# Attention with one set of products with v per head instead of two, a scaled negated maximum on ScalarE, and a last tile stored in two parts

## The chip, the cores and the metric

The kernel runs on one core of one Trainium2 chip. The metric is the device time in microseconds of one execution of the program. Five engines work side by side, each through its own queue of instructions in order: TensorE (PE, with its weight loads shown apart as PEld), VectorE (DVE), ScalarE (ACT), GpSimd (POOL) and SyncE (SP, which here only issues DMAs). They wait for one another through semaphores.

## What is computed

A trunk of two residual layers on 512 tokens of width 1024. Layer 0 mixes tokens with a gated linear attention, layer 1 with softmax attention; each is followed by a gated feed-forward block with a width-3 convolution over tokens. The change touches the softmax attention (8 query heads, 2 key/value heads, 128 wide) and the very last step of the second feed-forward block. The attention of the reference, cut:

```python
q = apply_rope(rmsnorm(q, q_norm), cos, sin)
k = apply_rope(rmsnorm(k, k_norm), cos, sin)
def block(q_blk):                       # 128 queries
    s = jnp.einsum('bkgqd,bksd->bkgqs', q_blk, k) * scale
    p = jax.nn.softmax(s, axis=-1)
    return jnp.einsum('bkgqs,bksd->bkgqd', p, v)
...
x = x + o @ w_out
x = x + conv_ffn(rmsnorm(x, norm_ffn[i]), ...)
```

## The kernel before

Everything is kept feature-major: a tile holds 128 features by 512 tokens. To keep float32 accuracy at the faster matmul type, each operand is split into a high part (rounded by an ACT copy) and a low part (the difference, made by DVE), and a product is three matmuls: high by high, high by low, low by high. `mm3` (line 251) issues these three, so lines 253 to 255 stand for most matmuls of the profile. Weights arrive as `raw` tiles of 1 MB on SP's queue; `Weights.make` (114) splits them by an ACT copy `wh` and a DVE subtraction `wl` (140, 141), or, for the attention's weights, by two ACT copies (123, 124) and an accumulating DMA that POOL issues (133). `wh` and `wl` have three buffers each.

A tile framework assigns buffers, inserts all waits, and reorders the instructions by its own cost model. The program's source order is thus only its priority; the order on each engine is what the built program shows. PSUM has eight banks, named by tag: `acc` (3), `s` (2), `pt` (2), `po` (1).

The attention (function `attention`, line 604) works by blocks of 128 queries, 32 blocks in all: four blocks (`j`) for each of eight heads (`h`). Block number t runs through these steps:

- `scores` (736): three matmuls of 512 columns give the scores `s` of 128 queries by 512 keys in an `s` bank. DVE takes the row maximum `mx` (745) and multiplies it by the row's scale and by -1 to `nb` (746). ACT computes exp with scale and bias `nb` into `p` and sums the row (748).
- `shares` (751): DVE takes the reciprocal `rc` of the sum (753) and scales `p` (754).
- `turn` (757), four blocks later: TensorE transposes the four 128x128 parts of `p` into a `pt` bank (766). ACT copies the bank to `pth` (769), DVE subtracts to `ptl` (770). A pair of these tiles holds two blocks: 4 key parts by 256 queries.
- `mix` (772), six blocks later and after every second block: twelve matmuls of 256 columns multiply v (`vh`, `vl`) with half a head's `pth`, `ptl` into one half of the `po` bank. After the second half, ACT and DVE split `po` into the head's output tile `oT` (670, 671).

Between these steps a plan (`Q_STEPS`, `Q_READY`, `O_STEPS`) places pieces of other work. These are the projections of the next pairs of query heads (`qpair`, 694, into `A` and `B`, with the head norms `hs` and `hr`, the scales `qsc`, the rotations `rt` on DVE and their sums `ry` on POOL at 663 and 664, and the split of `q` on ACT and DVE at 670 and 671), and the first parts of the output projection (`out_steps`, 292, into `op`). `hr` is a power on POOL (197).

The big tiles (`big`, 22 buffers) hold `pth`, `ptl`, `q`, `k` and the `oT` of heads 0 to 3; the `oT` of heads 4 to 7 use the eight `xhl` buffers that held the normalised input. The last feed-forward block adds each `dn` bank to the residual `x` on DVE (597) and stores it by a DMA on SP's queue (601).

Of the kernel before, what the change touches and what calls it, by code (L numbers as in the profile page):

```python
# [8 lines left out]
F32 = mybir.dt.float32  # L9
F32R = mybir.dt.float32r  # L10
U8 = mybir.dt.uint8
AF = mybir.ActivationFunctionType
ALU = mybir.AluOpType

P = 128
S = 512
D = 1024
KC = D // P
NT = S // P
# [12 lines left out]
LAGS = (4, 6)  # L32
# [14 lines left out]
def hybrid_encoder_kernel(  # L47
# [21 lines left out]
    pe, act, dve, pool, sync = nc.tensor, nc.scalar, nc.vector, nc.gpsimd, nc.sync  # L69
# [8 lines left out]
    def nm(s):  # L78
        uid[0] += 1
        return f"{s}{uid[0]}"  # L80
# [3 lines left out]
    def bank(tag, n):  # L84
        return pp.tile([P, S], F32, tag=tag, bufs=PS[tag], name=nm(n))

    def pair(tag, bufs, dt, n):
        return sp.tile([P, 2 * S], dt, tag=tag, bufs=bufs, name=nm(n))

    def big(dt, n):  # L90
        return pair("g", 22, dt, n)

    def tmp(tag, n, w=S):
        return sp.tile([P, w], F32, tag=tag, bufs={"u": 4, "t": 6, "sq": 3}[tag], name=nm(n))

    def tiny(w, n, tag="tiny"):
        return sp.tile([P, 8], F32, tag=tag, bufs={"tiny": 36, "tiny2": 4}[tag], name=nm(n))[:, :w]


    x = [cp.tile([P, S], F32, name=f"x{c}") for c in range(KC)]  # L100
# [150 lines left out]
    def mm3(ps, wh, wl, mh, ml, start, stop):  # L251

        mm(ps, wh, mh, start=start, stop=False)  # L253
        mm(ps, wh, ml, start=False, stop=False)  # L254
        mm(ps, wl, mh, start=False, stop=stop)  # L255
# [10 lines left out]
    def feature_tile(*a):  # L266
        for _ in feature_steps(*a):
            pass
# [290 lines left out]
    def ffn(layer, norm, cw, nxt):  # L559
        hl = []  # L560
        for m in range(FC):
            res, pss = [], []
            for t in range(2):
                ps = bank("s" if t else "acc", "up")
                feature_tile(*W.half(up[layer], 2 * m + t), norm.hl, ps)
                pss.append(ps)
                if m == 0 and t == 0:
                    norm.tokens()
                elif m == 0:
                    norm.rows()  # L570
            for t in range(2):
                ps = pss[t]
                cc = ((layer * 2 + t) * FC + m) * 4
                w = lambda i: cw[:, cc + i : cc + i + 1]
                u = tmp("u", "u")
                dve.tensor_tensor(u, ps, norm.R, ALU.mult)  # L576
                y = tmp("t", "y")
                act.activation(y, u, AF.Identity, scale=w(1), bias=w(3))  # L578
                dve.scalar_tensor_tensor(y[:, 1:], u[:, : S - 1], w(0), y[:, 1:], ALU.mult, ALU.add)  # L579
                dve.scalar_tensor_tensor(y[:, : S - 1], u[:, 1:], w(2), y[:, : S - 1], ALU.mult, ALU.add)  # L580
                res.append(y)
            act.activation(res[1], res[1], AF.Silu)  # L582
            dve.tensor_tensor(res[0], res[0], res[1], ALU.mult)
            t = big(F32R, "gu")
            act.activation(t[:, :S], res[0], AF.Copy)
            dve.tensor_tensor(t[:, S:], res[0], t[:, :S].bitcast(F32), ALU.subtract)
            hl.append((t[:, :S], t[:, S:]))
        cur = None
        for c in range(KC):
            ps = bank("acc", "dn")  # L590
            for k in range(FC):
                u = c * FC + k
                if u % 8 == 0:
                    cur = W.half(down[layer], u // 8)
                sl = slice((u % 8) * P, (u % 8 + 1) * P)
                mm3(ps, cur[0][:, sl], cur[1][:, sl], *hl[k], k == 0, k == FC - 1)
            dve.tensor_tensor(x[c], x[c], ps, ALU.add)
            if nxt is not None:
                nxt.chunk(c)
            else:  # L600
                sync.dma_start(out[c * P : (c + 1) * P, :], x[c])


    def attention(norm, nxt):
# [64 lines left out]
        def split(y, tile_):  # L669
            act.activation(tile_[:, :S], y, AF.Copy)  # L670
            dve.tensor_tensor(tile_[:, S:], y, tile_[:, :S].bitcast(F32), ALU.subtract)

        def whole(gen):
            while True:
                try:
                    next(gen)
                except StopIteration as e:
                    return e.value
# [39 lines left out]
        ps = [bank("acc" if j < 2 else "pt", "av") for j in range(NT)]  # L718
# [7 lines left out]
        vh, vl = big(F32R, "vh"), big(F32R, "vl")  # L726
        for j in range(NT):
            sl = slice(j * 256, (j + 1) * 256)
# [4 lines left out]
        oh = [None] * QH  # L733
        probs, pts, pos = {}, {}, {}

        def scores(h, j):

            qt, sc, e = heads[h]
            kt = kk[h // 4]
            js = slice(j * P, (j + 1) * P)  # L740
            s = bank("s", "s")
            mm3(s, qt[:, js], qt[:, S + j * P : S + (j + 1) * P], kt[:, :S], kt[:, S:], True, True)
            scj = sc[:, 2 * j + e : 2 * j + e + 1]
            mx, nb, sm, rc = (tiny(1, n) for n in ("mx", "nb", "sm", "rc"))
            dve.reduce_max(mx, s, axis=mybir.AxisListType.X)
            dve.tensor_scalar(nb, mx, scj, -1.0, ALU.mult, ALU.mult)
            p = tmp("t", "p")
            act.activation(p, s, AF.Exp, scale=scj, bias=nb, accum_out=sm)  # L748
            probs[h, j] = (p, sm, rc)

        def shares(h, j):
            p, sm, rc = probs[h, j]
            dve.reciprocal(rc, sm)
            dve.tensor_scalar(p, p, rc, None, ALU.mult)
            probs[h, j] = p

        def turn(h, j):

            hf, i = divmod(j, 2)
            if i == 0:  # L760
                pts[h, hf] = tuple(big(F32R, n).rearrange("p (k q) -> p k q", q=256) for n in ("pth", "ptl"))
            ph3, pl3 = pts[h, hf]
            p = probs.pop((h, j))
            tp = bank("pt", "pt")
            for k in range(NT):
                pe.transpose(tp[:, k * P : (k + 1) * P], p[:, k * P : (k + 1) * P], ident)  # L766
            isl = slice(i * P, (i + 1) * P)
            tp3 = tp.rearrange("p (k q) -> p k q", q=P)
            act.activation(ph3[:, :, isl], tp3, AF.Copy)
            dve.tensor_tensor(pl3[:, :, isl], tp3, ph3[:, :, isl].bitcast(F32), ALU.subtract)  # L770

        def mix(h, hf):
            ph3, pl3 = pts.pop((h, hf))
            vo = (h // 4) * HD
            if hf == 0:
                pos[h] = bank("po", "po")
            dst = pos[h][:, hf * 256 : (hf + 1) * 256]
            for k in range(NT):
                vsl = slice(k * 256 + vo, k * 256 + vo + HD)
                mm3(dst, vh[:, vsl], vl[:, vsl], ph3[:, k, :], pl3[:, k, :], k == 0, k == NT - 1)  # L780
            if hf == 1:
                t = big(F32R, "oT") if h < 4 else pair("xhl", 8, F32R, "oT")
                split(pos[h], t)
                oh[h] = (t[:, :S], t[:, S:])

        LAG, LAG2 = LAGS
        blocks = [(h, j) for h in range(QH) for j in range(NT)]
        osteps = out_steps(w_aout, oh, nxt)
        plan = collections.defaultdict(list)
# [4 lines left out]
                    plan[first + t] += [g] * n  # L794
        for t in O_STEPS:
            plan[t].append(osteps)
        for t in range(len(blocks) + LAG2):
            if t < len(blocks):
                scores(*blocks[t])
            for g in plan[t]:  # L800
                next(g, None)
            if LAG <= t < len(blocks) + LAG:
                turn(*blocks[t - LAG])
            if t < len(blocks):
                shares(*blocks[t])
            if t >= LAG2:
                h, j = blocks[t - LAG2]
                if j % 2 == 1:
                    mix(h, j // 2)
        whole(osteps)  # L810

    norms = [Norm(i) for i in range(4)]
    cw = gla(norms[0], norms[1])
    ffn(0, norms[1], cw, norms[2])
    attention(norms[2], norms[3])
    ffn(1, norms[3], cw, None)


# [79 lines left out]
```

## Time and profile before

| | before |
|---|---|
| median of 3 runs | 1140.84 us (1140.78 to 1142.55) |
| profiled execution | 1140.29 us |
| its span, first to last instruction | 1138.6 us |
| granted TensorE clock | 1.0 |
| PE / PEld / DVE / ACT / POOL busy | 99 / 83 / 60 / 42 / 7 % of the span |
| attention blocks, first scores to last product with v | 630.7 to 746.5 us |

The page of a profile gives busy time per engine, the span in 40 slices, the chain of work that ended last, and the costliest groups of instructions. A group's row reads: line, engine, operation, output <- inputs, shape, count, then busy us and mean ns of one, then idle time of the engine just before and what ended it. A timeline row reads: start in us from the span's start, duration, engine, line, operation, and in brackets the idle time before with its releaser. Matmuls are pipelined and their ends are modelled, so distances between their starts tell more than their durations.

### The profile page before, as it was taken

How to read it: one execution, taken by the hardware profiler on the slowest of the kernel's cores; microseconds unless marked ns; L12 is line 12 of the kernel's file. 1: busy time of each engine (PE TensorE's matmuls, PEld its weight loads, DVE VectorE, ACT ScalarE, POOL GpSimd, SP SyncE). 2: the span in 40 equal slices, each digit the busy share in tenths (PEclk: the TensorE clock that was granted, in tenths of full speed). 3: DMA queues.
4: the chain of work that ended last, by engine and by line, in shares of the span. 5: the costliest groups of instructions: out<-in, count | busy, mean ns of one | idle time of the engine just before them, and what ended most of it. 6: DMA issues, size and time to landing. Idle time of an engine off the chain costs nothing. (4 is left out here: it accounts for less than half of the span.)

```text
span 1138.6 us, 13034 instructions
## 1 busy us (share of the span) xinstructions
PE 1130.0 (99%) x5280; PEld 942.2 (83%) x5280; DVE 688.5 (60%) x996; ACT 481.7 (42%) x691; POOL 84.3 (7%) x73
## 2 busy tenths in 40 slices
PE   9999999999999999999999999999999999999998
PEld 8788888888888888888888888888888888888887
DVE  5677654567777777633325689756777777762221
ACT  6465233444444444422234666644444444441210
POOL 0214110000000000000004333000000000000000
PEclk9999999999999999999999999999999999999999
DMA  6322210222323223223247633222232322323320
GB/s 229 139 83 74 77 72 33 79 88 98 111 75 111 98 87 111 80 106 111 74 145 186 151 75 74 56 75 88 97 111 75 111 98 87 111 81 123 130 93 19
DMA packets 19836, 111.66 MB, mean 98 GB/s; under 512 B 2368, under 2 KB 2752, under 8 KB 8256
## 3 DMA queue, kind: packets, MB, share of 16 engines
q1 hardware_dynamic: 17328, 102.42, 25.8%
q0 software_dynamic: 2304, 8.39, 3.8%
q8 instruction: 41, 0.67, 0.2%
q14 instruction: 19, 0.16, 0.0%
q10 hardware_dynamic: 144, 0.02, 0.0%
HBM read 100.34 MB, written 2.10 MB: 90 GB/s over the span
## 5 line engine op out<-in xcount | busy, mean ns | idle before, releaser
L140 ACT ACTIVATE wh<-raw 128x1024 fp32r<-128x1024 f32 x164 | 173.0, 1056 | 337.9 <-PE up L254 132.0
L141 DVE TENSOR_TENSOR wl<-raw,wh 128x1024 fp32r<-128x1024 f32 x164 | 204.0, 1244 | 149.5 <-ACT wh L140 149.1
L253 PE MATMUL up<-xhl,wh 128*128 128x512 f32 x704 | 274.3, 390 | 0.0
L255 PE MATMUL up<-xhl,wl 128*128 128x512 f32 x704 | 274.0, 389 | 0.0
L254 PE MATMUL up<-xhl,wh 128*128 128x512 f32 x704 | 273.9, 389 | 0.0
L253 PEld LDWEIGHTS up<-xhl,wh 128*128 128x128 f32 x704 | 132.2, 188 | 27.5
L255 PEld LDWEIGHTS up<-xhl,wl 128*128 128x128 f32 x704 | 132.1, 188 | 27.4
L254 PEld LDWEIGHTS up<-xhl,wh 128*128 128x128 f32 x704 | 132.2, 188 | 27.2
L255 PE MATMUL dn<-gu,wl 128*128 128x512 f32 x352 | 136.9, 389 | 0.0
L253 PE MATMUL dn<-gu,wh 128*128 128x512 f32 x352 | 136.9, 389 | 0.0
L254 PE MATMUL dn<-gu,wh 128*128 128x512 f32 x352 | 136.9, 389 | 0.0
L576 DVE TENSOR_TENSOR u<-up,R 128x512 f32<-128x512 f32 x88 | 60.4, 688 | 52.3 <-PE up L255 52.2
L578 ACT ACTIVATE y<-u,cw 128x512 f32<-128x512 f32 x88 | 71.2, 812 | 21.7 <-DVE u L576 21.7
L255 PEld LDWEIGHTS dn<-gu,wl 128*128 128x128 f32 x352 | 66.1, 188 | 13.8
L253 PEld LDWEIGHTS dn<-gu,wh 128*128 128x128 f32 x352 | 66.1, 188 | 13.7
L254 PEld LDWEIGHTS dn<-gu,wh 128*128 128x128 f32 x352 | 66.1, 188 | 13.6
L308 PE MATMUL op<-oT,wh 128*128 128x512 f32 x256 | 70.5, 394 | 0.0
L580 DVE SCALAR_TENSOR_TENSOR y<-u,cw,y 128x511 f32<-128x511 f32 x88 | 65.9, 751 | 2.9
L579 DVE SCALAR_TENSOR_TENSOR y<-u,cw,y 128x511 f32<-128x511 f32 x88 | 65.6, 747 | 0.6 <-ACT y L578 0.6
L582 ACT ACTIVATE y<-y 128x512 f32<-128x512 f32 x44 | 27.9, 634 | 88.1 <-DVE y L580 88.0
L308 PEld LDWEIGHTS op<-oT,wh 128*128 128x128 f32 x256 | 47.2, 188 | 9.8 <-ACT p L748 0.3
L281 PE MATMUL vg<-wh,xhl 128*128 128x512 f32 x128 | 50.1, 396 | 0.2 <-ACT wh L140 0.2
(190 smaller groups left out, 1506.8 us busy)
## 6 DMA issues: line engine op xcount, KB each, us to landing
raw<-in_w_up_dram SPq DMA_DIRECT2D x44, 1024.0 KB, 4.8
raw<-in_w_down_dram SPq DMA_DIRECT2D x22, 1024.0 KB, 4.8
wl<-raw POOLq DMA_DIRECT2D x16, 512.0 KB, 4.7
raw<-in_w_vg_dram SPq DMA_DIRECT2D x6, 1024.0 KB, 4.8
raw<-in_w_akq_dram SPq DMA_DIRECT2D x5, 1024.0 KB, 5.1
raw<-in_w_kq_dram SPq DMA_DIRECT2D x4, 1024.0 KB, 4.7
raw<-in_w_gout_dram SPq DMA_DIRECT2D x4, 1024.0 KB, 4.7
raw<-in_w_aout_dram SPq DMA_DIRECT2D x4, 1024.0 KB, 4.7
```

Of the source, the lines that this page charges most:

```text
L140: act.activation(hi[:, sl], r[:, sl], AF.Copy)
L141: dve.tensor_tensor(lo[:, sl], r[:, sl], hi[:, sl].bitcast(F32), ALU.subtract)
L253: mm(ps, wh, mh, start=start, stop=False)
L254: mm(ps, wh, ml, start=False, stop=False)
L255: mm(ps, wl, mh, start=False, stop=stop)
L281: mm(ps[j][:, :width], xh, wh[:, sl], start=st, stop=False)
L308: mm(pss[ng][n], wt[:, sl], mv, start=k == 0 and i == 0, stop=k == KC - 1 and i == 2)
L576: dve.tensor_tensor(u, ps, norm.R, ALU.mult)
L578: act.activation(y, u, AF.Identity, scale=w(1), bias=w(3))
L579: dve.scalar_tensor_tensor(y[:, 1:], u[:, : S - 1], w(0), y[:, 1:], ALU.mult, ALU.add)
L580: dve.scalar_tensor_tensor(y[:, : S - 1], u[:, 1:], w(2), y[:, : S - 1], ALU.mult, ALU.add)
L582: act.activation(res[1], res[1], AF.Silu)
```

## The change

Four things change; layer 0, the projections and the plan stay.

1. `turn` now takes a head's four blocks into two pairs of tiles. A pair holds two key parts by all 512 queries. So a `pt` bank is copied by two ACT instructions and two DVE subtractions of 256 columns each, to the two pairs.
2. `mix` runs once per head, at the step at which its second half ran before: twelve matmuls of 512 columns into the whole `po` bank. There is no half-bank call two blocks earlier any more.
3. The maximum is taken negated by DVE, and the multiplication by the scale becomes an ACT copy with that scale, in place of the DVE instruction.
4. The last of the eight stored tiles is added and stored in two halves of 256 columns, the first on SP's DMA queue and the second on ACT's.

Besides, head 3's `oT` moves from the big tiles to the `xhl` buffers.

```diff
+                for sl, queue in ((slice(0, S // 2), sync), (slice(S // 2, S), act)):
+                    dve.tensor_tensor(x[c][:, sl], x[c][:, sl], ps[:, sl], ALU.add)
+                    queue.dma_start(out[c * P : (c + 1) * P, sl], x[c][:, sl])
...
-            dve.reduce_max(mx, s, axis=mybir.AxisListType.X)
-            dve.tensor_scalar(nb, mx, scj, -1.0, ALU.mult, ALU.mult)
+            dve.tensor_reduce(mx, s, axis=mybir.AxisListType.X, op=ALU.max, negate=True)
+            act.activation(nb, mx, AF.Copy, scale=scj)
...
-            hf, i = divmod(j, 2)
-            if i == 0:
-                pts[h, hf] = tuple(big(F32R, n).rearrange("p (k q) -> p k q", q=256) for n in ("pth", "ptl"))
-            ph3, pl3 = pts[h, hf]
+            if j == 0:
+                pts[h] = [[big(F32R, n).rearrange("p (k q) -> p k q", q=S) for n in ("pth", "ptl")] for _ in range(2)]
...
-            isl = slice(i * P, (i + 1) * P)
-            act.activation(ph3[:, :, isl], tp3, AF.Copy)
-            dve.tensor_tensor(pl3[:, :, isl], tp3, ph3[:, :, isl].bitcast(F32), ALU.subtract)
+            js = slice(j * P, (j + 1) * P)
+            for i, (ph3, pl3) in enumerate(pts[h]):
+                ks = slice(2 * i, 2 * i + 2)
+                act.activation(ph3[:, :, js], tp3[:, ks, :], AF.Copy)
+                dve.tensor_tensor(pl3[:, :, js], tp3[:, ks, :], ph3[:, :, js].bitcast(F32), ALU.subtract)
...
-        def mix(h, hf):
+        def mix(h):
...
+            po = bank("po", "po")
             for k in range(NT):
+                ph3, pl3 = pts[h][k // 2]
                 vsl = slice(k * 256 + vo, k * 256 + vo + HD)
-                mm3(dst, vh[:, vsl], vl[:, vsl], ph3[:, k, :], pl3[:, k, :], k == 0, k == NT - 1)
+                mm3(po, vh[:, vsl], vl[:, vsl], ph3[:, k % 2, :], pl3[:, k % 2, :], k == 0, k == NT - 1)
...
-                t = big(F32R, "oT") if h < 4 else pair("xhl", 8, F32R, "oT")
+            t = big(F32R, "oT") if h < 3 else pair("xhl", 8, F32R, "oT")
```

More of the change, by code (lines that the diff above doesn't have):

```diff
@@ L596, in ffn @@
                 mm3(ps, cur[0][:, sl], cur[1][:, sl], *hl[k], k == 0, k == FC - 1)
-            dve.tensor_tensor(x[c], x[c], ps, ALU.add)
-            if nxt is not None:
-                nxt.chunk(c)
-            else:
-                sync.dma_start(out[c * P : (c + 1) * P, :], x[c])
+            if nxt is not None or c < KC - 1:
+                dve.tensor_tensor(x[c], x[c], ps, ALU.add)
+                if nxt is not None:
+                    nxt.chunk(c)
+                else:
+                    sync.dma_start(out[c * P : (c + 1) * P, :], x[c])
+            else:
+                for sl, queue in ((slice(0, S // 2), sync), (slice(S // 2, S), act)):
+                    dve.tensor_tensor(x[c][:, sl], x[c][:, sl], ps[:, sl], ALU.add)
+                    queue.dma_start(out[c * P : (c + 1) * P, sl], x[c][:, sl])
     def attention(norm, nxt):
@@ L766, in turn @@
                 pe.transpose(tp[:, k * P : (k + 1) * P], p[:, k * P : (k + 1) * P], ident)
-            isl = slice(i * P, (i + 1) * P)
             tp3 = tp.rearrange("p (k q) -> p k q", q=P)
-            act.activation(ph3[:, :, isl], tp3, AF.Copy)
-            dve.tensor_tensor(pl3[:, :, isl], tp3, ph3[:, :, isl].bitcast(F32), ALU.subtract)
-        def mix(h, hf):
-            ph3, pl3 = pts.pop((h, hf))
+            js = slice(j * P, (j + 1) * P)
[4 more added lines that the diff above has]
+        def mix(h):
             vo = (h // 4) * HD
-            if hf == 0:
-                pos[h] = bank("po", "po")
-            dst = pos[h][:, hf * 256 : (hf + 1) * 256]
+            po = bank("po", "po")
             for k in range(NT):
+                ph3, pl3 = pts[h][k // 2]
                 vsl = slice(k * 256 + vo, k * 256 + vo + HD)
-                mm3(dst, vh[:, vsl], vl[:, vsl], ph3[:, k, :], pl3[:, k, :], k == 0, k == NT - 1)
-            if hf == 1:
-                t = big(F32R, "oT") if h < 4 else pair("xhl", 8, F32R, "oT")
-                split(pos[h], t)
-                oh[h] = (t[:, :S], t[:, S:])
-        LAG, LAG2 = LAGS
+                mm3(po, vh[:, vsl], vl[:, vsl], ph3[:, k % 2, :], pl3[:, k % 2, :], k == 0, k == NT - 1)
+            del pts[h]
+            t = big(F32R, "oT") if h < 3 else pair("xhl", 8, F32R, "oT")
+            split(po, t)
+            oh[h] = (t[:, :S], t[:, S:])
         blocks = [(h, j) for h in range(QH) for j in range(NT)]
@@ L796, in attention @@
             plan[t].append(osteps)
-        for t in range(len(blocks) + LAG2):
-            if t < len(blocks):
+        n = len(blocks)
+        for t in range(n + LAGS[1]):
+            if t < n:
                 scores(*blocks[t])
@@ L801, in attention @@
                 next(g, None)
-            if LAG <= t < len(blocks) + LAG:
-                turn(*blocks[t - LAG])
-            if t < len(blocks):
+            if LAGS[0] <= t < n + LAGS[0]:
+                turn(*blocks[t - LAGS[0]])
+            if t < n:
                 shares(*blocks[t])
[L806 to L809, printed above, removed]
+            h, j = divmod(t - LAGS[1], NT)
+            if h >= 0 and j == NT - 1:
+                mix(h)
         whole(osteps)
```

## The prediction

> **What bounds the kernel now.** First the page's busy line, then busy time by stretch for the thick of the attention, where nearly all of the change lies.
>
> ```profile
> PE 1130.0 (99%) x5280; PEld 942.2 (83%) x5280; DVE 688.5 (60%) x996; ACT 481.7 (42%) x691; POOL 84.3 (7%) x73
> ```
>
> ```profile
> 690.00:720.00 30.00, 29.07 (x182) 25.01 (x181) 27.11 (x64) 19.89 (x40) 7.92 (x6) 1.00 0.29 71
> ```
>
> In the second fence the columns are stretch, length, then busy us of PE, PEld, DVE, ACT, POOL. TensorE is nearly never without a matmul. So the change can win in two ways: shorter matmuls, or fewer stalls of PE; and it can lose by new stalls. Behind PE stand DVE (27.1 of 30 us) and ACT (19.9 of 30), with little slack in time: what counts is in which order each serves its queue. Ends of matmuls are modelled, so I read distances between starts. The timeline of PE:
>
> ```profile
> 713.18 0.39 PE L253 MATMUL s<-k,q 128*128 128x512 f32 x1
> ...
> 713.87 0.40 PE L308 MATMUL op<-oT,wl 128*128 128x512 f32 x1
> ...
> 714.78 0.28 PE L255 MATMUL po<-pth,vl 128*128 128x256 f32 x1
> ...
> 715.97 0.40 PE L253 MATMUL s<-k,q 128*128 128x512 f32 x1
> ```
>
> Three 512-column matmuls take 0.69 us, 0.230 each; ten 256-column ones 1.19 us, 0.119 each. Where the distance is longer, PE stood still. The waits of the attention and the longest stall:
>
> ```profile
> PEld s L253 <- ACT p L748: 2.3, 5, 1.0
> PEld s L255 <- DVE q L671: 0.7, 1, 0.7
> ```
>
> ```profile
> 709.72 0.28 PE L255 MATMUL po<-pth,vl 128*128 128x256 f32 x1
> 710.79 0.50 PE L253 MATMUL s<-k,q 128*128 128x512 f32 x1 [0.79 <-ACT p L748]
> ```
>
> The load queue waited 3.0 us in these two groups; taken as excess of start distances the loss is about 2.4 us, of which 1.07 - 0.12 = 0.95 is at 709.72. That is all that better feeding could give back.
>
> **The change part by part.**
>
> **Products with v.** 192 matmuls of 256 columns become 96 of 512: 192 x 0.119 = 22.8 us against 96 x 0.230 = 22.1, so **-0.8 us** (between -0.3 and -1.1, since distances of 0.227 to 0.234 occur). It stands wholly on PE's path. The Trainium skill, "TensorE: Matmul & The Clock Gate", section "Back-to-back issue gap", gives columns/2.4 plus 2.5 ns for a matmul alone; an estimate by that page is 96 x 2.5 ns = 0.24 us saved. The rows have 0.230 and 0.119 where that formula has 0.216 and 0.109, so here more is lost per instruction than it says.
>
> **The turned tile in two halves.** The groups by shape:
>
> ```profile
> L770 DVE TENSOR_TENSOR ptl<-pt,pth 128x512 fp32r<-128x512 f32 x32 | 21.9, 685 | 5.1 <-ACT pth L769 5.0
> L769 ACT ACTIVATE pth<-pt 128x512 fp32r<-128x512 f32 x32 | 19.0, 592 | 12.9 <-PE pt L766 12.7
> L748 ACT ACTIVATION_READ_ACCUMULATOR p<-s,nb,qsc 128x1 f32 x32 | 6.2, 195 | 0.0
> L730 DVE SCALAR_TENSOR_TENSOR vl<-av,rtok,vh 128x256 fp32r<-128x256 f32 x4 | 1.7, 478 | 2.1 <-ACT vh L729 2.1
> L729 ACT ACTIVATE vh<-av,rtok 128x256 fp32r<-128x256 f32 x4 | 1.6, 470 | 0.4 <-PE av L283 0.4
> ```
>
> Halves of 256 columns cost at most the 470 and 478 ns of L729 and L730 (these have a scalar operand besides): 0.94 for 0.59 on ACT, 0.96 for 0.69 on DVE per block. With about ten blocks in 30 us, DVE gets 2.7 and loses the 0.2 of nb ten times: 27.8 of 30. ACT gets 3.5 and nb (0.2 to 0.47, nearest the one-column 195 ns row plus a scalar: 0.25) 2.5: 25.9 of 30. So neither is over the bound; I cost the load itself at nothing, hidden under PE. Without that cover it would be 32 x 0.35 = 11 us. In the built program the second half on ACT waits for the first half's subtraction on DVE, so a bank passes ACT, DVE, ACT, DVE. The Trainium skill, "PSUM — Partial Sum Buffer", section "PSUM bank collisions raise a hardware error", says that two engines may not touch one bank at a time, reads included; the order of before, where ptl waits for pth anyway, cannot show it.
>
> **Negated maximum on ACT.** One round of the score loop, ACT then DVE:
>
> ```profile
> 712.07 0.78 ACT L748 ACTIVATE p<-s,nb,qsc 128x512 f32<-128x512 f32 x1 [0.85 <-DVE nb L746]
> ...
> 714.34 0.78 ACT L748 ACTIVATE p<-s,nb,qsc 128x512 f32<-128x512 f32 x1 [0.91 <-DVE nb L746]
> ```
>
> ```profile
> 712.97 0.17 DVE L753 RECIPROCAL rc<-sm 128x1 f32<-128x1 f32 x1 [0.34 <-ACT p L748]
> 713.05 0.67 DVE L745 TENSOR_REDUCE mx<-s 128x1 f32<-128x512 f32 x1
> 713.64 0.48 DVE L754 TENSOR_SCALAR p<-p,rc 128x512 f32<-128x512 f32 x1
> 714.03 0.21 DVE L746 TENSOR_SCALAR nb<-mx,qsc 128x1 f32<-128x1 f32 x1
> ```
>
> exp to rc 0.90, mx 0.08 later, then p sits between mx and nb: 2.27 us a round. Afterwards nb starts on ACT when mx ends (0.08 + 0.70) and takes about 0.28: 0.90 + 0.78 + 0.28 = 1.96. That can free some of the 2.4 us, no more. But nb now waits **in ACT's queue**: behind it stand exp, the halves of pth, oT, q and the weight copies.
>
> **What the new order does.** The scheduler has placed everything anew. I followed the built order from PE's waits back. Two places stand out, both where ACT copies q and must wait for GpSimd's ry. First pair (POOL, ACT, PE of before):
>
> ```profile
> 649.76 1.71 POOL L197 TENSOR_TENSOR hr<-hr,halfneg 128x8 f32<-128x8 f32 x1 [0.82 <-DVE rc L753]
> ...
> 655.65 1.30 POOL L664 TENSOR_TENSOR ry<-rt,rt 64x512 f32<-64x512 f32 x1
> ```
>
> ```profile
> 654.83 1.06 ACT L123 ACTIVATE wh<-raw 128x1024 fp32r<-128x1024 f32 x1 [0.61 <-PE A L254]
> 655.93 0.78 ACT L748 ACTIVATE p<-s,nb,qsc 128x512 f32<-128x512 f32 x1
> ...
> 657.65 1.16 ACT L670 ACTIVATE q<-ry 128x512 fp32r<-128x512 f32 x2
> ```
>
> ```profile
> 657.32 0.60 PE L766 MATMUL pt<-ident,p 128*128 128x128 f32 x4
> ...
> 659.18 0.40 PE L253 MATMUL s<-k,q 128*128 128x512 f32 x1
> ```
>
> ry is complete at 656.95. Before, the exp of block 6 (counted from 0) ran at 655.93, ahead of both q. After, ACT's order is q, half of pth, **q, half of pth, wh, nb, half of pth, exp of block 6**. So: second q at 656.98, next 0.52 later 657.50, half of pth 657.8, wh (about 0.96 to its successor) 658.75, nb and pth 0.35, exp at 659.1; its reader on PE comes 0.91 after an exp starts (709.88 to 710.79, below), at 660.0. PE has lost the po group that stood between 657.67 and 659.18 (it comes later, whole), so the scores of block 8, which need block 6's bank, would be due at 657.67. **+2.3 us**, of which about 1.0 falls already on the transposes of block 3, whose bank waits for the half of pth behind the second q.
>
> Last pair:
>
> ```profile
> 702.03 1.66 POOL L197 TENSOR_TENSOR hr<-hr,halfneg 128x8 f32<-128x8 f32 x1 [0.33 <-DVE hr L193]
> 703.67 2.85 POOL L663 TENSOR_TENSOR ry<-rt,rt 64x512 f32<-64x512 f32 x2
> 706.60 2.72 POOL L664 TENSOR_TENSOR ry<-rt,rt 64x512 f32<-64x512 f32 x2
> ```
>
> ```profile
> 699.99 0.95 PE L618 MATMUL hs<-bd,qa 128*128 128x2 f32 x8
> ```
>
> ```profile
> 709.35 0.63 ACT L670 ACTIVATE q<-ry 128x512 fp32r<-128x512 f32 x1 [0.80 <-POOL ry L664]
> 709.88 0.76 ACT L748 ACTIVATE p<-s,nb,qsc 128x512 f32<-128x512 f32 x1
> ```
>
> This made the 0.95 stall. After, GpSimd does one head's pair, then the other's: the first q is ready hr + 1.43 + 1.36 after hr starts, the second 2.8 later. hr started 1.1 us after PE's hs; now it has rc, mx and p (0.08 + 0.60 + 0.39) ahead, so 1.1 to 2.2. First q at 5.5 to 6.7, q, nb and exp's release 0.52 + 0.28 + 0.91: 7.2 to 8.4. PE's order from hs to the scores that need this exp holds two s (1.4), 8 po (1.84), three transposes (1.3) and 6 op (1.4): 5.9. Stall 1.3 to 2.5, I take 2.2; the second q gives another 0.7 (2.8 against 2.1 of PE's work). **+2.9** for 0.95.
>
> Middle pair:
>
> ```profile
> 676.01 1.26 DVE L625 SCALAR_TENSOR_TENSOR qsc<-hr,rtok 128x8 f32<-128x8 f32 x1
> ```
>
> qsc, waiting for hr and drawn out beside ry, now stands ahead of the subtractions that free the transposes' bank: 0.45 to 1.4, I take **+0.9**. After the first stall exp of block 7 is still late, **+0.3**; a weight copy of 1.06 us ahead of an exp near the end 0 to 0.9, **+0.5**.
>
> **Last tile in halves.** Timeline and DMA issues of the end:
>
> ```profile
> 1134.67 0.69 DVE L597 TENSOR_TENSOR x<-x,dn 128x512 f32<-128x512 f32 x1 [13.63 <-PE dn L255]
> 1135.39 0.33 SPq L601 DMA_DIRECT2D out_dram<-x  x1
> ```
>
> ```profile
> raw<-in_w_down_dram SPq DMA_DIRECT2D x5, 1024.0 KB, 4.8
> out_dram<-x SPq DMA_DIRECT2D x6, 256.0 KB, 2.0
> ```
>
> ```profile
> prm<-in_par_dram ACTq DMA_DIRECT2D x1, 22.0 KB, 3.1
> ```
>
> Two adds of 256 columns end some 0.06 later than one of 512; each DMA then moves half. 768 KB more take 2.8 us more, so 128 KB less save at most 0.47: between -0.4 and, as ACT's queue once took 3.1 to land, +1.1. Nearest is SP's row with the same tile: **-0.2**.
>
> Everything before the attention and the feed-forward layers keeps its instructions; one more oT in the xhl pool only moves one xhl copy, with over 4 us of PE's work ahead of its reader.
>
> **Sum.** -0.8 - 0.2 - 2.4 (old stalls) + 2.3 + 2.9 + 0.9 + 0.3 + 0.5 = +3.5 us. The profiled execution took 1140.29 (span 1138.6 and 1.7 around it), so 1143.8; the median of the runs shown is 0.55 above it: **1144.3**.
>
> **Rivals.** (a) *PE stays fed*: if ry or the copies come 2 to 3 us earlier than the rows say, or the shorter score loop (1.96 for 2.27) carries the rest, only -0.8, -0.2 and up to -2.4 remain: 1137.4 to 1139.8, say 1138.3. For it: the loop is shorter. Against: GpSimd's times repeat in every pair, and ACT serves in order. It decides where the first pair's exp ends before 657.7. (b) *One of the two q waits bites* and the old stalls go: -3.4 + 2.3 to 2.9 + 1.7 for the small ones: +0.6 to +1.2, say 1141.7. (c) *The bank becomes the bound*: four steps in turn with exp between them hold a bank 0.6 us longer per block at least; if 0.3 of it shows on PE in each of 32 blocks, +9.6 - 1.0: 1149. Against: two banks, with blocks 2.3 us apart or more, leave over 1 us. The rule of the Trainium skill's PSUM page above is why the four steps could not overlap.
>
> **How the numbers follow.** Chances: forecast 0.57, (a) 0.15, (b) 0.22, (c) 0.06. A change under 0.2% (2.3 us) can't be told from none: same is 1138.6 to 1143.1. The forecast's own span is 1142.4 to 1147.5 by its bounds, a tenth of it within 0.2%. So faster 0.11, same 0.30, slower 0.59. The range reaches from (a)'s upper part to above the forecast's bounds: 1139 to 1148.
>
> **What would show it.** Right: PE stalls of over 1 us at the transposes and scores of the first and last q pair, released by ACT behind a q that waits for POOL ry; po starts 0.23 apart. Wrong: these scores follow within 0.3 us; or stalls spread evenly over all blocks at the transposes, released by ptl (then (c)); or the last landing is over 2.2 us after its issue.

## The result and the profile after

| | before | after |
|---|---|---|
| median of 5 runs | 1140.78 us (1140.38 to 1142.55) | 1148.39 us (1148.19 to 1149.18) |
| span of the profiled execution | 1138.6 us | 1146.7 us |

The ratio is 1.0068 (95% interval 1.0057 to 1.0080): the change makes the kernel slower by 7.6 us. The forecast was 3.5 us more, 1144.3, in a range from 1139 to 1148.

First the page of after, its busy line; then busy time by stretch (stretch, length, PE, PEld, DVE, ACT, POOL, granted clock, DMA share, GB/s).

```profile
PE 1131.6 (99%) x5184; PEld 937.5 (82%) x5184; DVE 689.7 (60%) x997; ACT 492.7 (43%) x755; POOL 84.3 (7%) x73
```

```profile
630.00:660.00 30.00, 28.09 (x142) 23.03 (x140) 17.98 (x40) 19.38 (x38) 12.33 (x10) 1.00 0.57 140
660.00:690.00 30.00, 27.21 (x137) 22.07 (x138) 23.69 (x55) 22.04 (x56) 8.60 (x7) 1.00 0.29 72
690.00:720.00 30.00, 27.35 (x137) 21.98 (x135) 24.68 (x58) 21.14 (x54) 8.57 (x7) 0.94 0.28 70
```

The page alone hides the loss: PE's share is 99% before and after. The stretches show it: PE misses 2 to 3 us in each of the three, where it missed 0, 0.3 and 0.9 before, and in the third it was not granted its full clock. DVE has less work in each of the three than before (17.98 for 19.78, 23.69 for 24.81, 24.68 for 27.11 us). ACT has 1.3 less in the first and 2.8 and 1.3 more in the others, but some 8 of 30 us to spare at the least. So neither engine is full, and the lost time is waiting; the waits of the attention (630 to 770 us) name it, after first, before second:

```profile
ACT q L675 <- POOL ry L669: 7.1, 5, 2.8
PEld s L253 <- ACT p L753: 6.4, 7, 3.1
ACT pth L774 <- DVE ptl L775: 5.1, 7, 1.6
PE s L253 <- ACT p L753: 4.0, 4, 2.6
```

```profile
ACT q L670 <- POOL ry L664: 2.0, 2, 1.2
```

ScalarE stands 7.1 us for GpSimd's sums, 2.0 before; TensorE stands for exps on the same ScalarE; and a new wait, pth for ptl, is the bank going back and forth.

**The first pair of query heads** (timeline of after, POOL and ACT, then PE):

```profile
656.88 1.65 POOL L669 TENSOR_TENSOR ry<-rt,rt 64x512 f32<-64x512 f32 x1
658.56 0.63 ACT L675 ACTIVATE q<-ry 128x512 fp32r<-128x512 f32 x1 [2.23 <-POOL ry L669]
659.10 0.36 ACT L774 ACTIVATE pth<-pt 128x256 fp32r<-128x256 f32 x1
659.36 1.05 ACT L123 ACTIVATE wh<-raw 128x1024 fp32r<-128x1024 f32 x1
660.31 0.28 ACT L751 ACTIVATE nb<-mx,qsc 128x1 f32<-128x1 f32 x1
660.76 0.78 ACT L753 ACTIVATE p<-s,nb,qsc 128x512 f32<-128x512 f32 x1
```

```profile
658.45 0.39 PE L255 MATMUL B<-xhl,wl 128*128 128x512 f32 x1
660.07 0.63 PE L769 MATMUL pt<-ident,p 128*128 128x128 f32 x4 [1.23 <-DVE ptl L775]
661.68 0.50 PE L253 MATMUL s<-k,q 128*128 128x512 f32 x1 [0.98 <-ACT p L753]
```

The bracket 2.23 is ScalarE doing nothing; none of the four rows below it has a wait of its own. PE then starts 1.62 us after B instead of 0.23, and 1.61 after the transposes instead of 0.35 (as from 657.32 to 657.67 before): 2.6 us.

**The middle pair:**

```profile
680.30 2.60 POOL L668 TENSOR_TENSOR ry<-rt,rt 64x512 f32<-64x512 f32 x2
680.35 1.24 DVE L630 SCALAR_TENSOR_TENSOR qsc<-hr,rtok 128x8 f32<-128x8 f32 x1 [1.02 <-POOL hr L197]
680.41 0.39 PE L253 MATMUL po<-pth,vh 128*128 128x512 f32 x1
681.51 0.74 DVE L775 TENSOR_TENSOR ptl<-pt,pth 128x256 fp32r<-128x256 f32 x2
681.95 0.38 ACT L774 ACTIVATE pth<-pt 128x256 fp32r<-128x256 f32 x1 [1.59 <-DVE ptl L775]
682.39 0.63 PE L769 MATMUL pt<-ident,p 128*128 128x128 f32 x4 [1.59 <-DVE rc L758]
```

VectorE waits 1.02 us for hr, then takes 1.24 us for eight columns beside ry; behind it stand the two subtractions ptl, which end at 682.25 and give the transposes their bank. The bracket of the transposes names rc, VectorE's next instruction, but rc belongs to a later block: its p is scaled only at 683.16. PE loses 1.98 - 0.23 = 1.75 us.

**The last pair**, VectorE and GpSimd, then ACT, then PE:

```profile
707.44 0.42 DVE L775 TENSOR_TENSOR ptl<-pt,pth 128x256 fp32r<-128x256 f32 x1 [0.92 <-ACT pth L774]
707.79 0.16 DVE L193 TENSOR_SCALAR hr<-hs 128x8 f32<-128x8 f32 x1
708.10 1.66 POOL L197 TENSOR_TENSOR hr<-hr,halfneg 128x8 f32<-128x8 f32 x1 [1.05 <-DVE hr L193]
```

```profile
712.45 0.63 ACT L675 ACTIVATE q<-ry 128x512 fp32r<-128x512 f32 x1 [2.76 <-POOL ry L669]
712.99 0.28 ACT L751 ACTIVATE nb<-mx,qsc 128x1 f32<-128x1 f32 x1
713.30 0.78 ACT L753 ACTIVATE p<-s,nb,qsc 128x512 f32<-128x512 f32 x1
```

```profile
714.23 0.50 PE L253 MATMUL s<-k,q 128*128 128x512 f32 x1 [2.65 <-ACT p L753]
...
716.04 1.20 PE L308 MATMUL op<-oT,wh 128*128 128x512 f32 x2
717.04 0.66 PE L253 MATMUL s<-k,q 128*128 128x512 f32 x1
...
719.16 0.63 PE L308 MATMUL op<-oT,wl 128*128 128x512 f32 x2
```

A stall of 2.8 us (start to start) after q, nb and exp. The chain behind q starts late already: GpSimd's hr starts 2.6 us after the end of hs (704.56, lasting 0.95), since the step before it on VectorE (L193) stands behind a ptl that waited 0.92 us for ScalarE's pth. And then there is something that the prediction had no term for: the seven matmuls that start from 716.04 on, up to the one at 719.16, take 3.12 us where 7 x 0.230 = 1.61 is due. The windows tell why, with the granted clock in the third column from the right:

```profile
714.00:716.00 2.00, 1.77 (x9) 1.46 (x10) 1.79 (x6) 1.56 (x7) 1.10 (x1) 0.92 0.00 0
716.00:718.00 2.00, 2.00 (x7) 1.43 (x6) 1.73 (x6) 1.70 (x6) 0.00 (x0) 0.50 0.00 0
718.00:720.00 2.00, 2.00 (x11) 1.61 (x9) 1.36 (x4) 0.86 (x2) 0.00 (x0) 0.73 0.00 0
```

After the stall the clock was halved for 3.4 us: 1.5 us more.

**The end** (timeline of after):

```profile
1142.63 0.39 PE L255 MATMUL dn<-gu,wl 128*128 128x512 f32 x1
1143.06 0.75 DVE L605 TENSOR_TENSOR x<-x,dn 128x256 f32<-128x256 f32 x2 [13.63 <-PE dn L255]
```

From this last matmul to the end of the span are 1146.7 - 1142.63 = 4.07 us; before, the add that follows it started at 1134.67, 0.42 after the matmul at 1134.25, and to 1138.6 were 4.35. So -0.28 at the end, and 1142.63 - 1134.25 = 8.38 ahead of it. Of these 0.49 are there before the change can matter (the third matmul to A in the score loop starts at 633.16, before at 632.67); I did not follow them. The other 7.9 arise from 633 to 760; after that both traces run in step.

### The profile page after: what moved, and what is told of

Read it like the earlier page. It is cut to its first block, busy times and chain, and to the rows that moved or that the text cites. A ratio compares the mean times of both kernels' runs of the same rounds, so it can differ in the third digit from the quotient of the medians.

```text
span 1146.7 us, 12918 instructions
## 1 busy us (share of the span) xinstructions
PE 1131.6 (99%) x5184; PEld 937.5 (82%) x5184; DVE 689.7 (60%) x997; ACT 492.7 (43%) x755; POOL 84.3 (7%) x73
## 4 chain that ended last, share of the span: by engine, by line
PE 94%; ACT 2%; DVE 2%; POOL 1%; issue 0%; DMA 0%; SPq 0%; DVEq 0%; POOLq 0%; ACTq 0%
PE up L253 14%; PE up L255 14%; PE up L254 14%; PE op L308 7%; PE dn L254 7%; PE dn L253 7%; PE dn L255 7%; PE vg L282 2%; PE vg L283 2%; PE vg L281 2%; PE o L521 2%; PE pt L769 1%; PE kv L500 1%; PE k L255 1%; PE k L254 1%; PE k L253 1%
## 5 line engine op out<-in xcount | busy, mean ns | idle before, releaser
L282 PE MATMUL vg<-wl,xhl 128*128 128x512 f32 x128 | 50.0, 391 | 0.1
```

The lines of the kernel that those rows point to most:

```text
L282: mm(ps[j][:, :width], xh, wl[:, sl], start=False, stop=False)
```

## The experiments

Seventeen kernels gave a time (e4, a first form of e5, gave none), each beside the kernel before on the same chip (its medians there: 1140.50 to 1140.70). "Theory Q" is the prediction's: q, waiting for GpSimd, stands ahead of exps on ScalarE. "H" or "M" blames the halves or the products as such, "F" the work that was taken from between the scores. Each edit has the framework place all instructions anew, so a run shows what its whole built order does, not the named part in isolation.

### One part alone

**e1, the last tile in halves.** Edit: only the `+` lines of the store loop.

> The kernel before with only the last tile sent in halves. All theories: the last matmul starts where it did, and from there to the end of the span 4.35 us become 4.1 (4.07 in the profile of after), so -0.3 us on 1140.8. If it is 0 or above, the two profiles differ in their ends by chance.

1140.21 us, ratio 0.9997 (0.9989 to 1.0006), span 1138.3: 0.3 less, as expected, and not to be told from nothing by the times.

**e2, the negated maximum on ScalarE.** Edit: only `tensor_reduce(..., negate=True)` and `act.activation(nb, ...)`.

> The kernel before with only the negated maximum scaled on ScalarE; products with v and tail as before. Theory Q (ScalarE copies q, which waits for GpSimd's ry, ahead of exps, and what stands behind is late): in this built order both q of the first pair and of the second stand ahead of nb, a pth and an exp, in the last pair q, pth, nb, q, exp; so PE stalls at the scores behind them, 1.5 to 3 us at the first pair and about 2 at the last, and the time is 1143 to 1146. Theory M (the products with v, 12 matmuls at once per head and the turned tile in halves, starve PE): nb alone shortens the score loop and loses nothing, 1138.5 to 1140.8.

1140.03 us, ratio 0.9995 (0.9986 to 1.0004). What I expected from the order of the built program was wrong: q stands ahead of nb and an exp there, too, but the waits of the attention hold no line of ScalarE's q on ry at all. By the time ScalarE comes to q, ry is there. This part costs one thing, a wait of PE for qa, whose second square comes late in ScalarE's longer queue; the waits of e2:

```profile
PEld hs L618 <- DVE qa L636: 1.4, 2, 1.2
```

PE's start is 0.90 us late there, and the same stall (0.91) is in after at 648. In e2 the old stalls of 0.95, 0.44 and 0.40 are gone, and besides the one at hs there is one of 0.89, at scores that wait for q's low part: 1.8 us lost in both. That the shorter score loop took the old ones away is likely, but not shown.

**e3, the products with v.** Edit: `turn`, `mix` and the loop's last lines; nb and the store as before.

> The kernel before with only the products with v changed (512 columns per head, turned tile in halves, later mix); nb on VectorE and tail as before. Theory Q: q of the first pair stands ahead of two exps, of the second pair ahead of one, of the last ahead of an exp; stalls as in after but without the nb behind q: 1143 to 1147, and the stalls stand at the three q pairs, in few large pieces. Theory M: nearly the whole +7.6 is here, 1147 to 1149, with stalls at transposes and scores of blocks without a q as well.

1146.84 us, ratio 1.0053 (1.0040 to 1.0065). So 6.3 of the 7.6 us are here, with nb where it was. Its waits:

```profile
ACT q L670 <- POOL ry L664: 9.1, 6, 3.2
```

The wait is there without nb on ScalarE, and no smaller than in after (7.1). Stalls of 1.9 (at the transposes of the first pair) and 2.5 us (at the scores of the last) lead the list, as Q says; pieces of 0.3 to 0.5 at eight other places speak for a smaller share of M.

### Which part of the products, and is it the order?

**e5, q later in the changed kernel.** An order edge, no work changed:

```diff
-                split(ys[e], t)
+                with tc.issue_after(exps[-2].ins) if i else ExitStack():
+                    split(ys[e], t)
...
-            act.activation(p, s, AF.Exp, scale=scj, bias=nb, accum_out=sm)
+            exps.append(act.activation(p, s, AF.Exp, scale=scj, bias=nb, accum_out=sm))
```

> The changed kernel with nothing but an order edge: each copy of q on ScalarE is put behind the exp that was emitted one step before (for the three q pairs inside the score loop). Theory Q (q, waiting for GpSimd's ry, stands ahead of exps and holds them up): the stalls of the first pair (1.39 + 1.15 + 0.31 us in the profile of after) and of the last (2.81, and the 1.5 that PE then loses at a lower granted clock) go or shrink to under 1 us each, the one of 1.75 in the middle stays: 1142 to 1144.5. If q is then late for its own scores, stalls of 1 to 2 us released by q instead: 1145 to 1147. Theory M (the products with v as such): 1147.5 to 1149.

1142.36 us, ratio 1.0015 (1.0006 to 1.0024): 6.0 of the 7.6 us go with an edge on ScalarE alone. The first pair's stalls shrink to 0.39, the last's to 0.72, the clock stays at 1.00, and ScalarE's q has no wait for ry in the list. The middle one is there unchanged (1.75).

**e6, the halves alone.** The turned tile per head in halves as in the change, the products as before (12 of 256 columns, twice per head):

```diff
+                ph3, pl3 = (a[:, k % 2, hf * 256 : (hf + 1) * 256] for a in pts[h][k // 2])
+                mm3(dst, vh[:, vsl], vl[:, vsl], ph3, pl3, k == 0, k == NT - 1)
```

> The kernel before with only the turned tile made in halves per head; the products with v stay 256 columns wide, 12 at a time, twice per head, as early as before. On ScalarE its order at the first pair is that of the kernel with the products alone (half of pth, q, exp, half of pth, q, weights, exp), on TensorE the products stand between the same scores as before. Theory Q/halves (ScalarE's order, q ahead of exps): 1144 to 1147, stalls at the first and last pair as with the products alone. Theory F (fill: the products were TensorE's work while q was on its way, and moving them took it away): at most 1142.5.

1147.15 us (1145.37 to 1148.52; the profile is of the slowest run), ratio 1.0054 (1.0040 to 1.0068). ScalarE at the first pair:

```profile
654.58 0.63 ACT L670 ACTIVATE q<-ry 128x512 fp32r<-128x512 f32 x1 [3.18 <-POOL ry L664]
655.12 0.76 ACT L748 ACTIVATE p<-s,nb,qsc 128x512 f32<-128x512 f32 x1
...
657.64 0.63 ACT L670 ACTIVATE q<-ry 128x512 fp32r<-128x512 f32 x1 [1.40 <-POOL ry L664]
```

The framework, with two short copies in place of one, puts q ahead of an exp that ran at 652.86 before. So 6.6 of the 7.6 us come with the halves alone, though the products with v stand where they stood.

**e7, the later time alone.** All 24 products of a head at the step where the change has its 12, nothing else.

> The kernel before with only the time of the products changed: all 24 of a head (256 columns each) are issued where the changed kernel has its 12; the turned tile is made whole as before and ScalarE has q where it had it before. Theory F (fill): 1144 to 1147, stalls at the scores and transposes of the first and last pair, where the products no longer stand. Theory Q/halves: within 1.5 us of before, 1139.5 to 1142.5.

1141.91 us, ratio 1.0011 (1.0003 to 1.0020): +1.3. Taking the products from between the scores costs a little (single stalls of 1.49 and 0.88), not the 3 to 6 us that F asked for.

**e8, the products one step later still** in the changed kernel: `LAGS = (4, 7)`.

> The changed kernel with the products with v one step later still (second lag 7 instead of 6). In the built order hs of the second and third pair stand one group of matmuls earlier against their scores. Theory F: what counts is TensorE's work between hs and the scores behind q; the second and last pair gain 1 to 3 us, the first, whose order is unchanged, nothing: 1144.5 to 1147.5. Theory Q alone says no change beyond 1 us, since q still stands ahead of nb and exp: 1147.5 to 1149.5.

1144.49 us, ratio 1.0037 (1.0025 to 1.0050). The first pair keeps its two stalls (1.41 and 1.26, in after 1.39 and 1.26); the middle's 1.75 becomes 0.60, the last's 2.81 becomes 1.75. F's range was met and Q's was not; but the built order of q moved as well (qa and a copy of weights came ahead of it), so this run doesn't part the two.

### What is it about q, and what about the bank?

**e9, q ahead of an exp in the kernel before.** `tc.add_manual_dep(exps[-3].ins, c.ins.name, edge, ...)`, where `c` is ScalarE's copy to q.

> The kernel before, nothing of the change in it, with order edges alone: on ScalarE, the exp emitted two steps before a copy of q (of the three pairs inside the score loop) is put behind that q. So ScalarE's order at the first pair has q ahead of the exp of block 5, as the kernel with halves alone has it, while the turned tile stays whole. Theory Q (the order is the price): 1144 to 1148, ScalarE waiting 5 us and more for POOL ry, stalls of 2 us and more at the scores of the first and last pair. Theory H (the halves' own time and their two turns of the bank are the price): within 1 us of before.

1139.62 us, ratio 0.9993 (0.9985 to 1.0002). Q, as I had put it, is wrong here:

```profile
656.18 0.59 ACT L634 ACTIVATE qa<-A 128x512 f32<-128x512 f32 x1
656.65 0.63 ACT L670 ACTIVATE q<-ry 128x512 fp32r<-128x512 f32 x1
657.17 0.79 ACT L752 ACTIVATE p<-s,nb,qsc 128x512 f32<-128x512 f32 x1
```

q is ahead of the exp but has no bracket: other copies had moved ahead of it, and ry was ready. An order that never makes ScalarE stand costs nothing. **e15** tried again, with a weight copy behind q as well:

> The kernel before with order edges alone, as in the run that took 1139.62, where q went ahead of an exp but never came to wait for GpSimd, since a weight copy and turned tiles had moved ahead of it. Here the weight copy emitted last is behind q as well, so that q comes up on ScalarE before ry is there. If the price is ScalarE standing still for ry with exps behind it, whatever the turned tile looks like: q waits 2 us or more in all, 1143 to 1147, stalls at the scores of the first or last pair. If it takes the halves to make the wait cost: 1139.5 to 1141.5 though q waits.

1140.39 us, ratio 0.9997 (0.9988 to 1.0005), and again q did not wait. So it does not answer what it was made for.

**e10, halves alone with q later** (the edge of e5).

> The turned tile in halves alone (products 256 wide, early, as in the run with halves alone that took 1147.15), plus the order edge that puts each q behind the exp emitted one step before. Theory Q: nearly all of the 6.6 us goes, 1140.5 to 1142. Theory H: 1145.5 or more stays.

1143.45 us, ratio 1.0025 (1.0015 to 1.0034): 3.7 of 6.6 go, 2.9 stay. Neither theory had this. No stall is over 0.9 now, but there are eleven of 0.2 to 0.9, and the waits hold

```profile
ACT pth L770 <- DVE ptl L771: 8.2, 11, 1.9
```

**e13, the same with the halves grouped**, so that the bank changes hands once, as before the change:

```diff
             for i, (ph3, pl3) in enumerate(pts[h]):
                 act.activation(ph3[:, :, js], tp3[:, 2 * i : 2 * i + 2, :], AF.Copy)
+            for i, (ph3, pl3) in enumerate(pts[h]):
                 dve.tensor_tensor(pl3[:, :, js], tp3[:, 2 * i : 2 * i + 2, :], ph3[:, :, js].bitcast(F32), ALU.subtract)
```

> The run with halves alone and q later (1143.45) with one thing changed: the two halves are copied one after the other on ScalarE and then subtracted one after the other on VectorE, so the bank changes hands once and not three times. If the 2.9 us that are left over before are the bank's turns (my rival c in a smaller size): 1140.8 to 1141.8, and ScalarE's pth waits for ptl no more. If they are the extra time of the halves on VectorE and ScalarE (0.13 and 0.07 us each per block): 1142.8 to 1144.

1140.09 us, ratio 0.9994 (0.9985 to 1.0003). That is below its range. The wait of pth for ptl is gone from the list and so are the 3.4 us. The halves' longer copies by themselves cost nothing that shows.

**e17, grouped, q left where the framework puts it**; **e18, the changed kernel, grouped**.

> Halves of the turned tile alone (1147.15), copied in pairs so that the bank changes hands once; q is left where the scheduler puts it, which is ahead of the exp of block 5 as with halves alone. It closes a table of two by two with e6 (three turns, q early: 1147.15), e10 (three turns, q later: 1143.45) and e13 (one turn, q later: 1140.09). If q's place is a price of its own: 1142.5 to 1145, ScalarE waits 3 us and more for POOL ry and the stalls of 1.9 and 2.9 us at the first and last pair are there. If it costs only together with the bank's turns: 1139.7 to 1141.5.

> The changed kernel with the halves grouped and nothing else; q where the scheduler puts it, ahead of nb and exp. If q's place is a price of its own: 1143 to 1146.5, with the stalls of the first and last pair. If the bank's turns are the root: 1139.5 to 1141.5.

1146.71 us, ratio 1.0053 (1.0040 to 1.0065), and 1147.90, ratio 1.0073 (1.0059 to 1.0087). e17's ScalarE:

```profile
654.13 0.63 ACT L670 ACTIVATE q<-ry 128x512 fp32r<-128x512 f32 x1 [4.00 <-POOL ry L664]
654.67 0.76 ACT L748 ACTIVATE p<-s,nb,qsc 128x512 f32<-128x512 f32 x1
```

That closes the table for the halves alone (before: 1140.6):

| | bank changes hands 3 times | once |
|---|---|---|
| q where the framework puts it | 1147.15 (e6) | 1146.71 (e17) |
| q behind the exp | 1143.45 (e10) | 1140.09 (e13) |

With one hand-over, q's place is worth 6.6 us. Not all of that follows straight from ScalarE's wait. In e17 the wait of 4.00 is followed by stalls of only 0.58 and 0.65 at the first pair, where 1.9 were expected. The last pair has 2.40 and, behind it, a stretch at half clock; the middle pair has 0.94 at hs, for a late qa, and later scores 0.82. Both e17 and e18 lie above their ranges.

The hand-overs are worth 3.4 us with q later. With q early e6 and e17 differ by 0.4, less than e6's own runs differ from each other (1145.37 to 1148.52), so there it can't be told from nothing.

### The middle pair, and the best versions

**e11, q later and qsc later** in the changed kernel: besides e5's edge, `with tc.issue_after(ptls[-1].ins)` around `scale_end`'s instruction.

> The changed kernel with q put later as in the run that took 1142.36, and also qsc (the small VectorE product that waits for GpSimd's hr and was drawn out to 1.24 us beside ry) put behind the subtraction ptl emitted last before it. My term C says that the stall of 1.75 us at the transposes of the middle pair comes from qsc standing ahead of ptl: it goes, 1140.3 to 1141.3. If ptl was late for another reason, or nb of the next head then waits for qsc: 1142 to 1143.

1140.81 us, ratio 1.0002 (0.9993 to 1.0011), 1.55 less than e5. PE's busy time from 660 to 690, e5 first, e11 second:

```profile
660.00:690.00 30.00, 28.41 (x145) 22.97 (x144) 24.20 (x57) 22.00 (x55) 8.60 (x7) 1.00 0.29 71
```

```profile
660.00:690.00 30.00, 29.52 (x151) 24.14 (x150) 25.75 (x60) 23.34 (x57) 8.67 (x7) 1.00 0.29 71
```

The 1.75 are gone (0.65 at the scores of the next head came instead). So two order edges, one on ScalarE and one on VectorE, take the whole loss back.

**e14, with the halves grouped besides; e16, with nb back on VectorE too; e12, the kernel before with nb, the last tile in halves, and the squares at high priority.**

> The changed kernel with q later, qsc later (1140.81) and the halves grouped as in the run beside it. If the bank's turns cost 1 to 3 us there as well: 1138.3 to 1139.8, faster than both kernels. If they do not: 1140.3 to 1141.3.

> As the run with halves grouped, q and qsc later, but the scaled negated maximum back on VectorE as before. With nb on ScalarE, TensorE waited 0.93 us at hs for qa in every run; that goes (-0.9), the longer score loop (2.27 us a round for an estimated 1.96) may cost up to 1: within 1 us of the run beside it, 1138 to 1140.5.

> The kernel before with two parts of the change, the negated maximum scaled on ScalarE and the last tile in halves, and with the two squares of A and B and their sum ahead of other ready work (high priority), since with nb on ScalarE PE waited 0.90 us at hs for qa. 1140.03 - 0.34 - 0.9 = 1138.8 if that wait goes and nothing else moves; 1139.7 if the squares were late anyway; above 1140.5 if what they overtake (nb, exp) is then late.

e14: 1139.92, ratio 0.9993 (0.9984 to 1.0001). That lies between its two ranges: the grouping gains 0.9 us on e11, and the intervals of the two overlap. e16: 1140.69, 0.9998 (0.9989 to 1.0007), 0.2 above its range; hs is on time there, but the scores of the middle pair wait 1.24 for q. e12: 1139.69, 0.9992 (0.9983 to 1.0000), as its second case has it; the squares were late all the same (0.93 at hs). None beats the kernel before by what can be told; all three beat the changed one by 7 us and more.

## Why the prediction was right in its direction and wrong in its size

- **Products with v, -0.8.** Borne out by the rows: the new ones start 0.23 apart (733.74, 733.97, 734.20 and on to 735.12 in after), 96 x 0.230 for 192 x 0.119.
- **Last tile, -0.2.** Measured -0.28.
- **Old stalls, -2.4.** They go, but the three single ones (0.95, 0.44, 0.40) are 1.8 in start distances. I had summed two groups of waits of the load queue.
- **First pair, +2.3, and the exp of the next block, +0.3.** Measured 2.6 and 0.31, at the transposes and scores named, through the very queue named.
- **Middle pair, +0.9.** Right place and mechanism (e11), wrong size: 1.75. Its bounds were 0.45 to 1.4. The prediction says that qsc waits for hr and is drawn out beside ry; the two are 1.02 and 1.24 us, more together than its price allows for.
- **Last pair, +2.9.** The first stall is 2.8, for 2.2 with bounds of 1.3 and 2.5. The mis-sized link is the start of hr: 2.6 us after hs, where the prediction had 1.1 to 2.2 and did not count that VectorE would wait for ScalarE's half of pth ahead of it. The second stall (0.7) does not show, because TensorE was then at half clock and lost 1.5 us; that this term was too large by about as much as the first was too small is luck. 4.3 in all.
- **Negated maximum on ScalarE.** The prediction listed what stands behind nb: "exp, the halves of pth, oT, q and the weight copies". It left out the squares of A and B, which hs waits for: 0.91 in after for 0.07 before, +0.8; e2 has it with nb alone.
- **Weight copy near the end, +0.5.** A copy of 1.06 us does stand ahead of an exp, at 727.69; three pieces of 0.24, 0.18 and 0.34 follow between 729 and 732, 0.76 in all.

By these: -0.8 - 0.3 - 1.8 + 2.6 + 0.3 + 1.75 + 4.3 + 0.8 + 0.8 = +7.65, and with the 0.49 at the start 8.1, which is what the spans differ by (a single term is good to about 0.1). The mechanism, q on ScalarE waiting for GpSimd with exps behind it, was right. The step that failed is the sizing in the sum: the middle pair (1.75 for 0.9), the first stall of the last pair (2.8 for 2.2), and two terms put at nothing, the clock after the last stall (1.5) and hs waiting for the squares (0.8).

Two readings behind the terms were wrong as well. First, the prediction took nb on ScalarE to be part of what holds exps up ("nb now waits in ACT's queue"): alone it costs no time on balance (e2), and most of the loss is there without it (6.3 us in e3). Second, it counted the products that had moved ("PE has lost the po group") as what exposes the wait: moved alone they cost 1.3 (e7), and left in place they do not help (e6). What counts is that the halves led the framework to issue q before ry is there. Rival (c), the bank in four steps, had 0.06 and 9.6 us; it is real at 3.4 us (e10 against e13), but covered in the changed kernel (0.5 from after to e18, 0.9 from e11 to e14). The argument against it, over 1 us of spare time for two banks, holds on the mean, not where several copies queue up.

Open: why the framework's cost model prefers q early with the halves, and whether the wait would cost as much with the turned tile whole, since neither e9 nor e15 made q wait.

## What to carry to other kernels

When an instruction is split on an engine that serves in order, look at what the scheduler moved past the pieces: find the instructions there that wait for a slower engine, and price the whole time that the engine stands, wait and drawn-out work together. Test it with an order edge before taking the change back; here two edges returned the 7.6 us. And when two small instructions share a bank with another engine's, issue them as a group, so that the bank changes hands once.

## What the hardware showed that I had not expected

A stall of TensorE well under 3 us can cost twice. After idle times of 2.65 us (after), 2.74 (e6), 2.24 (e17) and 3.94 (e18) the granted clock fell to 0.50 for 3.41 us (6.83 in e6); after 2.34 us in e3 it did not. What seems to decide is how the idle time falls into stretches of 3.41 us: in the records of the clock in these traces every change lies a whole number of 3.413 us after the first. Here are such stretches, of e17, then of e3:

```profile
707.73:711.14 3.41, 1.41 (x9) 0.89 (x7) 2.12 (x4) 1.20 (x3) 3.26 (x3) 1.00 0.00 0
711.14:714.56 3.42, 3.18 (x10) 2.60 (x11) 2.88 (x7) 1.36 (x5) 1.37 (x2) 0.50 0.00 0
```

```profile
707.59:711.00 3.41, 2.43 (x13) 1.69 (x11) 2.92 (x6) 0.62 (x2) 3.26 (x4) 1.00 0.19 36
711.00:714.41 3.41, 2.04 (x11) 1.73 (x12) 2.07 (x7) 2.66 (x7) 2.52 (x2) 1.00 0.00 0
714.41:717.82 3.41, 3.41 (x19) 2.81 (x18) 3.29 (x10) 2.29 (x8) 0.00 (x0) 1.00 0.00 0
```

In e17 TensorE is idle for 2.00 of the 3.41 us, and the next stretch has half the clock. In e3 a border parts the stall: 0.98 and 1.37 us are idle, and neither is followed by a fall. The other three that were followed by one have 1.96 us (after), 1.98 (e6) and 2.93 (e18); in the attention the most that was not is 1.72 (e6, from 657.80). So the 1.5 us depend in part on chance. In e3's five runs the two with a mean clock of 1.000 took 1145.63 and 1145.94 us, the three with 0.999 1146.84 to 1147.17; only the run of 1145.94 has a profile, so that the same fall is behind this is likely, not shown.

The Trainium skill, "TensorE: Matmul & The Clock Gate", section "Part 1: The HAM clock gate (the "warmup" mystery)", gives half rate after an idle window of about 3.4 us and calls the window free-running. The half rate and the length agree with these traces. That the window has to be idle as a whole does not: 1.96 of 3.41 us were enough.

VectorE is drawn out beside GpSimd not only in tiny instructions. In after the scaling of p takes 1.50 us at 709.80, where ry runs on POOL (709.74 to 711.01), against 0.48 elsewhere:

```profile
709.74 1.27 POOL L668 TENSOR_TENSOR ry<-rt,rt 64x512 f32<-64x512 f32 x1
709.80 1.50 DVE L759 TENSOR_SCALAR p<-p,rc 128x512 f32<-128x512 f32 x1
```
